# One decoder layer in fp32: the t3 splits ahead of the first pair's products, and the down projection in groups of 2, 3, 4, 3, 4, 3, 3

## The chip, the core and the metric

The kernel runs on one core of one Trainium2 chip. The core has a matrix engine (PE), a vector engine (DVE), a scalar engine (ACT), a general engine (POOL) and a queue that issues DMA (SP). Each engine takes its own instructions in the order of the program, and they wait for one another through semaphores. The metric is the device time of one execution in microseconds (us).

## The reference

The layer modulates x, adds two attention mixers, and then does what matters here: a gated feed-forward block with a residual and a layer norm.

```python
u = x * (1.0 + scale_f) + shift_f                  # (1024, 1024)
h = jnp.einsum('btd,df->btf', u, w_gate_up)        # 2 x 2816 columns
hg, hu = jnp.split(h, 2, axis=-1)
y = jnp.einsum('btf,fd->btd', jax.nn.silu(hg) * hu, w_down)
x = layer_norm(DEEPNORM_ALPHA * x + (1.0 + gate_f) * y, ln2_g, ln2_b)
```

Everything is float32.

## The kernel before

A float32 product is made from rounded halves. An operand is split into a high part (ACT copies it to fp32r) and a low part (DVE subtracts the high part from the operand), and a product takes three matmuls: high with high, high with low, low with high. A split is thus one ACT and one DVE instruction, and both must be done before the matmuls that read it.

The 2816 hidden columns are 22 blocks of 128, called f or p. The program has two stages here.

**Gate and up, 22 pairs p.** For each pair the gate and up columns come from seven products of half size instead of eight (a Strassen-like scheme). `PRODUCTS = ("b11", "b21", "t2", "t1", "t3", "b22", "t4")` names the seven right-hand operands, i = 0 to 6. Each is an array of four 128-row blocks k, with a high and a low tile (t3h and t3l, and so on). They are made once, around the first pair, from the normalised activations: `late_input(k)` and `late_rest(name, k)` make and split block k. The left-hand operand of product i of pair p is a combination of weight halves, split by `g_split(p, i)` into w_hi and w_lo, four buffers each. POOL makes the combinations in `g_sums(p, step)`. Each product is 12 matmuls over four blocks k. For pairs 0 to 2, products 0 and 1 are made ahead of the loop over p; the first pair's products 2 to 6 are the first work of that loop, and the DVE and ACT instructions of `late_rest` stand between them. `g_prepare(upto)` splits the weights of the next products ahead of their use. The result of pair p is stored to HBM (h_d).

**Down, groups of f.** `groups = [3] * 6 + [4]` are the numbers of blocks f in a group. For each group, for each of eight row blocks tb and each of two halves eh, PE sums 3 matmuls per f into one PSUM bank (`ps_f` has six banks), and DVE adds the bank to the sum zt in SBUF (line 1326). While a group runs, the arrays of the next one are made at certain row blocks: `h_prepare(f)` splits h, which `h_load(f)` fetched from HBM, and two `ws.step()` split the two halves of w_down of that f. A `ws.step()` has POOL multiply the raw weights by the gate (line 62), ACT and DVE split them (lines 78 and 79), and SP fetch a later piece into one of three raw buffers. The first group's arrays are made during the last pair (p = 21). Groups alternate between two pools of big tiles, `bigu` with 8 and `low` with 6; an f takes two tiles.

In the last group DVE also takes the statistics of each finished row block and applies the norm (`half_stats`, `moments`, `norm_shared`; `norm_quick` for the last block). The line that decides at which row blocks arrays are made is

```python
if todo and tb % 2 == 0 or len(todo) > 3 - tb // 2 and todo:
```

that is row blocks 0, 2, 4 for three blocks f and 0, 2, 4, 6 for four.

Of the kernel before, what the change touches and what calls it, by code (L numbers as in the profile page):

```python
# [98 lines left out]
def decoder_layer(ctx: ExitStack, tc: tile.TileContext, I, out, dbg=None):  # L99
    nc = tc.nc  # L100
# [83 lines left out]
            add_chunk(I["w_o"][eh, kp], 2, 1, lambda eh=eh: gates[2][:, eh * 512:(eh + 1) * 512],  # L184
                      pair_dest(late, kp, lambda kp: "low", "o_hl") if eh else None)
    ws.limit = len(ws.jobs)
    down_pool = lambda f: "low" if min(f // 3, 6) % 2 else "bigu"
    for f in range(NF):
        for c in range(2):
            ws.add(I["w_down"][f * P:(f + 1) * P, c * 512:(c + 1) * 512], 1,  # L190
# [904 lines left out]
    def g_split(p, i):  # L1095
        hi, lo = [wpool.tile([P, 512], F32R, name=s, tag=s, bufs=4) for s in ("w_hi", "w_lo")]
        split(hi, lo, g_source(p, i))
        ready.append((hi, lo))
# [60 lines left out]
    def late_rest(name, k):  # L1159
        r12, r22 = late[k]  # L1160
        if name == "t1":
            split_to("t1", k, raw11[:, k])
            nc.gpsimd.tensor_tensor(r12, r22, r12, op=OP.subtract)
        elif name == "t3":
            split_to("t3", k, r12)
        elif name == "b22":
            split_to("b22", k, r22)
        else:
            split_to("t4", k, raw21[:, k])
# [20 lines left out]
            early_gate(k // 2)  # L1190
    late_rest("t1", 3)
    g_split(0, 3)


    jobs = [(p, i) for p in range(NF) for i in range(2 if p < EARLY_PAIRS else 0, 7)]
    prepared = [2]

    def g_prepare(upto):
        while prepared[0] < min(upto, len(jobs)):
# [4 lines left out]
            prepared[0] += 1  # L1204


    groups = [3] * 6 + [4]
    hs, h_raw = {}, {}

    def h_load(f):  # L1210
# [8 lines left out]
    for p in range(NF):  # L1219
        ps = dict(zip("ab", acc.pop(p))) if p in acc else {}  # L1220
        if p == 1:
            x2_ctx.close()
            ev = ctx.enter_context(tc.tile_pool(name="ev", bufs=1, side="right", reuse_waits="tile"))
        s, g = {}, [None, None]

        def kept(name):
            if p:
                return ev.tile([P, TH], F32, name=name, bufs=4 if name == "g" else 1)
            return x2p.tile([P, TH], F32, name="r", tag="r", bufs=6)

        for i in range(7):
            if p == 0 and i == 2:
                late_rest("t3", 0)
                early_gate(2)
            elif (p, i) in jobs:
                g_prepare(n + 3)
            bank = "abacaca"[i]
            if bank not in ps:
                ps[bank] = ps_f.tile([P, TH], F32, name="pf")
            if (p, i) in jobs:  # L1240
                product(ps[bank], i, i in (0, 1, 3))
                n += 1
            x = ps[bank]
            if i in (0, 2):
                g[i // 2] = gated.get(p) if i == 0 else None
                if not g[i // 2]:
                    g[i // 2] = kept("g")
                    nc.scalar.activation(g[i // 2], x, AF.Copy)
            if p == 0 and i == 2:
                for k in range(1, 4):  # L1250
                    late_rest("t3", k)
                operand("t4", low)
                g_prepare(n + 2)
            if i in (3, 4):
                s[i] = kept(f"c{i}")
                nc.scalar.activation(s[i], x, AF.Copy)
            if i in (1, 5):
                t = i // 5
                if t or p not in gated:
                    nc.vector.tensor_tensor(g[t], g[t], x, op=OP.add)  # L1260
                nc.scalar.activation(g[t], g[t], AF.Silu)
            if i == 4:
                nc.gpsimd.tensor_tensor(s[4], s[4], s[3], op=OP.add)
            if i == 6:
                nc.vector.tensor_tensor(g[0], g[0], x, op=OP.mult)
                nc.vector.tensor_tensor(g[1], g[1], s[4], op=OP.mult)
                for t in range(2):
                    nc.sync.dma_start(h_d[p][:, t * TH:(t + 1) * TH], g[t])
            if p == 0 and i in (3, 4):
                for k in range(4):  # L1270
                    if i == 3:
                        nc.vector.tensor_tensor(raw21[:, k], raw21[:, k], raw_t2[:, k], op=OP.subtract)
                    late_rest({3: "b22", 4: "t4"}[i], k)
            if p + 1 < NF:
                if i == 4 and p + 2 < NF:
                    g_load(p + 2)
                if i in (2, 3, 4):
                    g_sums(p + 1, i - 2)
                if p == NF - 2 and i == 5:
                    ws.limit = None  # L1280
                    ws.send()
            else:
                if i == 0:
                    h_load(0)
                    h_load(1)
                    for j in range(3):
                        ws.scale(len(ws.done) + j)
                if i in (2, 3, 4):
                    h_prepare(i - 2)
                    if i == 2:  # L1290
                        h_load(2)
                for _ in range({2: 2, 3: 1, 5: 1, 6: 2}.get(i, 0)):
                    ws.step()
            if p == EARLY_PAIRS and i == 0:
                gb1 = norm_params(1)
            if i == 6 and EARLY_PAIRS <= p < EARLY_PAIRS + NB:
                gain(p - EARLY_PAIRS, gb1)
# [4 lines left out]
    for gi, n in enumerate(groups):  # L1302
        fs = range(f0, f0 + n)
        f0 += n
        last = gi == len(groups) - 1
        todo = [] if last else list(range(f0, f0 + groups[gi + 1]))
        for f in todo[:2]:
            if f not in h_raw:
                h_load(f)
        for tb in range(NB):  # L1310
            c = slice(tb * P, (tb + 1) * P)
            if todo and tb % 2 == 0 or len(todo) > 3 - tb // 2 and todo:
                f = todo.pop(0)
                h_prepare(f)
                ws.step()
                ws.step()
                if len(todo) > 1:
                    h_load(todo[1])
            for eh in range(2):
                es = slice(eh * 512, (eh + 1) * 512)  # L1320
                pd = ps_f.tile([P, TH], F32, name="pf")
                for i, f in enumerate(fs):
                    wd, h = wd_t[f][0], hs[f]
                    mac(pd, (h[:, 0, c], h[:, 1, c]), (wd[:, 0, es], wd[:, 1, es]), i == 0, i == n - 1)
                z = zrow(tb)[:, es]
                nc.vector.scalar_tensor_tensor(z, z, ALPHA if gi == 0 else 1.0, pd, op0=OP.mult, op1=OP.add)  # L1326
                if last:
                    half_stats(tb, eh)
                    if eh == 0 and tb:
                        ends.pop(0)()  # L1330
            if last:
                if tb == NB - 1:
                    norm_quick(tb, gb2, out)
                else:
                    ends.append(norm_shared(tb, gb2, out))
# [77 lines left out]
```

## Time and profile before

| | |
|---|---|
| median of 3 runs | 1901.1 us (1900.1 to 1901.41) |
| the profiled execution, its own time | 1908.77 us |
| its span from the first to the last instruction | 1907.0 us |
| mean granted TensorE clock | 0.987 of full |
| PE busy | 1841.1 us (97%) |
| DVE / ACT / POOL busy | 1160.4 / 782.0 / 596.5 us |

The profiled execution is 7.7 us longer than the median of the runs without a profile. Times below are microseconds from the start of its span. Matmuls overlap, so the step from one start to the next tells the rate, not the duration of one.

### The profile page before, as it was taken

The page shows a single profiled execution, that of the slowest core. Times are in us where ns is not written, and L with a number is a line of the kernel's source. Part 1 is how long each engine was busy: PE and PEld are TensorE (multiplying, and loading weights), DVE is VectorE, ACT ScalarE, POOL GpSimd, SP SyncE. Part 2 cuts the span into 40 slices and gives each one's busy share as a digit, 9 for nine tenths or more (in the row PEclk, how much of TensorE's full clock was granted, in tenths as well). Part 3 has the DMA queues.
Part 4 walks back from the last instruction along what each step waited for, and adds up shares of the span by engine and source line. Part 5 has one row for each costly group of instructions (what it writes and reads, how often), then busy time and mean ns, then how long its engine had stood idle before and what let it go on. Part 6 is the DMA issues. An engine that isn't in the chain of part 4 may idle for free.

```text
span 1907.0 us, 24471 instructions
## 1 busy us (share of the span) xinstructions
PE 1841.1 (97%) x8988; PEld 1489.6 (78%) x8988; DVE 1160.4 (61%) x2161; ACT 782.0 (41%) x1661; POOL 596.5 (31%) x389
## 2 busy tenths in 40 slices
PE   6899999999999999989999999999999999899998
PEld 5688877878878777768888878778888888788886
DVE  7855667667677887534555364575565444565557
ACT  3455545445444767633122132653333333412122
POOL 2432223223323222100311142455664333431213
PEclk9899999999999999989999999999999999999999
DMA  8011112111121122254534123123222222432222
GB/s 316 28 34 34 40 41 74 45 57 56 41 63 50 53 89 68 79 178 164 175 118 161 56 75 124 56 89 100 89 78 89 78 89 95 135 125 90 93 71 89
DMA packets 72266, 170.83 MB, mean 90 GB/s; under 512 B 13073, under 2 KB 14161, under 8 KB 72146
## 3 DMA queue, kind: packets, MB, share of 16 engines
q1 hardware_dynamic: 71810, 168.21, 26.7%
q8 instruction: 71, 1.16, 0.3%
q0 software_dynamic: 336, 1.06, 0.2%
q14 instruction: 49, 0.40, 0.1%
HBM read 145.80 MB, written 23.43 MB: 89 GB/s over the span
## 4 chain that ended last, share of the span: by engine, by line
PE 51%; DVE 3%; ACT 1%; issue 1%; DMA 1%; SPq 0%; POOL 0%; DVEq 0%; ACTq 0%; POOLq 0%
PE pf L1106 21%; PE p L138 5%; PE p L139 5%; PE p L137 5%; PE pf L137 5%; PE pf L139 5%; PE pf L138 5%; DVE m L118 1%; DMA h_raw<-h_d 0%; DVE wd L79 0%; DVE h L118 0%; DMA oa_d<-o 0%; PE px L1034 0%; PE p L835 0%; PE p L842 0%
## 5 line engine op out<-in xcount | busy, mean ns | idle before, releaser
L137 PE MATMUL pj<-u,w_hi 128*128 128x512 f32 x720 | 301.5, 419 | 0.0
L139 PE MATMUL pj<-u,w_lo 128*128 128x512 f32 x720 | 283.9, 394 | 0.0
L138 PE MATMUL pj<-u,w_hi 128*128 128x512 f32 x720 | 282.6, 392 | 0.0
L425 POOL TENSOR_TENSOR rb<-rb,sin_t 128x512 f32<-128x512 f32 x64 | 86.8, 1356 | 502.0 <-DVE rb L423 431.5
L118 DVE TENSOR_TENSOR w_lo<-r,w_hi 128x512 fp32r<-128x512 f32 x110 | 117.7, 1072 | 138.7 <-ACT w_hi L117 137.9
L79 DVE TENSOR_TENSOR w_lo<-w_raw,w_hi 128x512 fp32r<-128x512 f32 x150 | 133.4, 893 | 85.3 <-ACT w_hi L78 83.0
L528 ACT ACTIVATE probs<-probs,st 128x128 f32<-128x128 f32 (+1 forms) x320 | 146.0, 461 | 60.5 <-DVE st L518 30.8
L137 PEld LDWEIGHTS pj<-u,w_hi 128*128 128x128 f32 x720 | 136.4, 189 | 33.6 <-issue 4.7
L139 PEld LDWEIGHTS pj<-u,w_lo 128*128 128x128 f32 x720 | 135.8, 189 | 30.7
L138 PEld LDWEIGHTS pj<-u,w_hi 128*128 128x128 f32 x720 | 136.7, 190 | 22.6
L137 PE MATMUL pf<-wd,h 128*128 128x512 f32 x352 | 139.2, 395 | 3.4 <-DVE zt L1326 2.9
L138 PE MATMUL pf<-wd,h 128*128 128x512 f32 x352 | 138.7, 394 | 1.9 <-DVE wd L79 1.9
L139 PE MATMUL pf<-wd,h 128*128 128x512 f32 x352 | 138.6, 394 | 0.0
L62 POOL TENSOR_TENSOR w_raw<-w_raw,gate 128x512 f32<-128x512 f32 x60 | 83.1, 1404 | 157.0 <-DMA w_raw<-in_w_down 134.4
L1326 DVE SCALAR_TENSOR_TENSOR zt<-zt,pf 128x512 f32<-128x512 f32 x112 | 76.2, 685 | 85.1 <-PE pf L139 85.0
L426 POOL TENSOR_TENSOR r<-ra,rb 128x512 f32<-128x512 f32 x63 | 114.5, 1817 | 6.1 <-DVE kl L460 1.3
L78 ACT ACTIVATE w_hi<-w_raw 128x512 fp32r<-128x512 f32 x150 | 92.0, 624 | 29.0 <-PE p L138 12.0
L552 ACT ACTIVATE ptsb<-pt 128x512 f32<-128x512 f32 (+1 forms) x128 | 63.6, 548 | 93.6 <-PE pt L550 93.2
L137 PE MATMUL p<-u,w_hi 128*128 128x512 f32 x224 | 88.3, 394 | 0.0
L139 PE MATMUL p<-u,w_lo 128*128 128x512 f32 x224 | 87.2, 389 | 0.0
L138 PE MATMUL p<-u,w_hi 128*128 128x512 f32 x224 | 87.2, 389 | 0.0
L137 PE MATMUL p<-o_hl,w_hi 128*128 128x512 f32 x192 | 75.9, 395 | 8.0 <-ACT o_hl L117 8.0
(297 smaller groups left out, 4267.2 us busy)
## 6 DMA issues: line engine op xcount, KB each, us to landing
w_raw<-in_w_in SPq DMA_DIRECT2D x118, 256.0 KB
r<-in_w_gate_up SPq DMA_DIRECT2D x47, 512.0 KB
a_raw<-in_w_ada SPq DMA_DIRECT2D x32, 512.0 KB
w_raw<-in_w_down SPq DMA_DIRECT2D x44, 256.0 KB
h_raw<-h_d SPq DMA_DIRECT2D x22, 512.0 KB
h_d<-g SPq DMA_DIRECT2D x40, 256.0 KB
wa<-in_w_ada_m SPq DMA_DIRECT2D x16, 512.0 KB
wb<-wt_d SPq DMA_DIRECT2D x24, 256.0 KB
```

The source lines that it names most:

```text
L62: self.nc.gpsimd.tensor_tensor(self.raws[i], self.raws[i], scale(), op=OP.mult)
L78: self.nc.scalar.activation(hi, raw, AF.Copy)
L79: self.nc.vector.tensor_tensor(lo, raw, hi, op=OP.subtract)
L118: nc.vector.tensor_tensor(lo, src, hi, op=OP.subtract)
L137: nc.tensor.matmul(ps, w[0], m[0], start=first, stop=False)
L138: nc.tensor.matmul(ps, w[0], m[1], start=False, stop=False)
L139: nc.tensor.matmul(ps, w[1], m[0], start=False, stop=last)
L425: eng.tensor_tensor(b, b, sin_t[:, s], op=OP.mult)
L426: eng.tensor_tensor(residue_half(res, r, t), by_residue(a, r), by_residue(b, r), op=OP.add)
L528: nc.scalar.activation(pr, pr, AF.Exp, bias=st[:, 0, h, b:b + 1], accum_out=st[:, 1, h, b:b + 1])
L1106: nc.tensor.matmul(ps, w[:, c], m[:, k], start=first and k == 0 and n == 0, stop=k == 3 and n == 2, skip_group_check=True)
L1326: nc.vector.scalar_tensor_tensor(z, z, ALPHA if gi == 0 else 1.0, pd, op0=OP.mult, op1=OP.add)
```

## The change

Three things are changed. First, the four splits of t3, and the weight split of product 4 of pair 0, stand before the loop over pairs, so ahead of the first pair's products 2 and 3 in the program; before, one t3 split stood ahead of product 2 and three behind it. Second, the first Silu of pair 0 stands behind that of its second half (i = 5). Third, the down groups are 2, 3, 4, 3, 4, 3, 3, the last pair makes the arrays of two blocks f instead of three (and loads the raw h of blocks 2 and 3), and the next group's arrays are made at row blocks 1, 3, 5 for three and 1, 2, 4, 6 for four.

```diff
--- before.py
+++ after.py
@@ -184,7 +184,8 @@
             add_chunk(I["w_o"][eh, kp], 2, 1, lambda eh=eh: gates[2][:, eh * 512:(eh + 1) * 512],
                       pair_dest(late, kp, lambda kp: "low", "o_hl") if eh else None)
     ws.limit = len(ws.jobs)
-    down_pool = lambda f: "low" if min(f // 3, 6) % 2 else "bigu"
+    groups = [2, 3, 4, 3, 4, 3, 3]
+    down_pool = lambda f: "low" if sum(f >= e for e in np.cumsum(groups)) % 2 else "bigu"
     for f in range(NF):
         for c in range(2):
             ws.add(I["w_down"][f * P:(f + 1) * P, c * 512:(c + 1) * 512], 1,
@@ -1190,10 +1191,15 @@
             early_gate(k // 2)
     late_rest("t1", 3)
     g_split(0, 3)
+    for k in range(2):
+        late_rest("t3", k)
+    g_split(0, 4)
+    for k in range(2, 4):
+        late_rest("t3", k)
 
 
     jobs = [(p, i) for p in range(NF) for i in range(2 if p < EARLY_PAIRS else 0, 7)]
-    prepared = [2]
+    prepared = [3]
 
     def g_prepare(upto):
         while prepared[0] < min(upto, len(jobs)):
@@ -1204,7 +1210,6 @@
             prepared[0] += 1
 
 
-    groups = [3] * 6 + [4]
     hs, h_raw = {}, {}
 
     def h_load(f):
@@ -1230,7 +1235,6 @@
 
         for i in range(7):
             if p == 0 and i == 2:
-                late_rest("t3", 0)
                 early_gate(2)
             elif (p, i) in jobs:
                 g_prepare(n + 3)
@@ -1247,10 +1251,7 @@
                     g[i // 2] = kept("g")
                     nc.scalar.activation(g[i // 2], x, AF.Copy)
             if p == 0 and i == 2:
-                for k in range(1, 4):
-                    late_rest("t3", k)
                 operand("t4", low)
-                g_prepare(n + 2)
             if i in (3, 4):
                 s[i] = kept(f"c{i}")
                 nc.scalar.activation(s[i], x, AF.Copy)
@@ -1258,7 +1259,10 @@
                 t = i // 5
                 if t or p not in gated:
                     nc.vector.tensor_tensor(g[t], g[t], x, op=OP.add)
-                nc.scalar.activation(g[t], g[t], AF.Silu)
+                if p or t:
+                    nc.scalar.activation(g[t], g[t], AF.Silu)
+            if p == 0 and i == 5:
+                nc.scalar.activation(g[0], g[0], AF.Silu)
             if i == 4:
                 nc.gpsimd.tensor_tensor(s[4], s[4], s[3], op=OP.add)
             if i == 6:
@@ -1285,11 +1289,10 @@
                     h_load(1)
                     for j in range(3):
                         ws.scale(len(ws.done) + j)
-                if i in (2, 3, 4):
-                    h_prepare(i - 2)
-                    if i == 2:
-                        h_load(2)
-                for _ in range({2: 2, 3: 1, 5: 1, 6: 2}.get(i, 0)):
+                if i in (2, 4):
+                    h_prepare(i // 2 - 1)
+                    h_load(i // 2 + 1)
+                for _ in range({2: 2, 3: 1, 5: 1}.get(i, 0)):
                     ws.step()
             if p == EARLY_PAIRS and i == 0:
                 gb1 = norm_params(1)
@@ -1304,12 +1307,13 @@
         f0 += n
         last = gi == len(groups) - 1
         todo = [] if last else list(range(f0, f0 + groups[gi + 1]))
+        prepare_at = {0: (), 3: (1, 3, 5), 4: (1, 2, 4, 6)}[len(todo)]
         for f in todo[:2]:
             if f not in h_raw:
                 h_load(f)
         for tb in range(NB):
             c = slice(tb * P, (tb + 1) * P)
-            if todo and tb % 2 == 0 or len(todo) > 3 - tb // 2 and todo:
+            if tb in prepare_at:
                 f = todo.pop(0)
                 h_prepare(f)
                 ws.step()
```

DVE at the first pair. Names are those of the tiles (w_lo is the low part of a weight, raw and raw_t are the unsplit t4 and t2). Before:

```order
L118 TENSOR_TENSOR w_lo<-s_10415,w_hi 128x512
L1047 TENSOR_TENSOR t3l<-r,t3h 128x512
L1175 TENSOR_TENSOR spare<-spare,pf 128x512
L1047 TENSOR_TENSOR t3l<-r,t3h 128x512 x2
L1047 TENSOR_TENSOR t3l<-spare,t3h 128x512
L118 TENSOR_TENSOR w_lo<-r_10350,w_hi 128x512
L118 TENSOR_TENSOR w_lo<-r_10348,w_hi 128x512
L1272 TENSOR_TENSOR raw_10061<-raw_10061,raw_t_10487 128x512
```

and with the change:

```order
L118 TENSOR_TENSOR w_lo<-s_10415,w_hi 128x512
L1048 TENSOR_TENSOR t3l<-r,t3h 128x512 x2
L118 TENSOR_TENSOR w_lo<-r_10350,w_hi 128x512
L1048 TENSOR_TENSOR t3l<-r,t3h 128x512
L1048 TENSOR_TENSOR t3l<-spare,t3h 128x512
L1176 TENSOR_TENSOR spare<-spare,pf 128x512
L118 TENSOR_TENSOR w_lo<-r_10348,w_hi 128x512
L1276 TENSOR_TENSOR raw_10061<-raw_10061,raw_t_10487 128x512
```

The same eight rows of work stand there; the weight split of product 4 (w_lo<-r_10350) is third or fourth instead of sixth, and the addition that reads PSUM (spare<-spare,pf) comes last of the moved ones.

DVE at the end of the last pair and in the first down group, before:

```order
L118 TENSOR_TENSOR h<-h_raw,h 128x1024
L1260 TENSOR_TENSOR g<-g,pf 128x512
L79 TENSOR_TENSOR wd<-w_raw,wd 128x512
L1265 TENSOR_TENSOR g<-g,pf 128x512
L1266 TENSOR_TENSOR g<-g,c_13717 128x512
L79 TENSOR_TENSOR wd<-w_raw,wd 128x512 x2
L118 TENSOR_TENSOR h<-h_raw,h 128x1024
L79 TENSOR_TENSOR wd<-w_raw,wd 128x512 x2
L1326 SCALAR_TENSOR_TENSOR zt<-zt,pf 128x512 x4
```

and with the change:

```order
L118 TENSOR_TENSOR h<-h_raw,h 128x1024
L1261 TENSOR_TENSOR g<-g,pf 128x512
L79 TENSOR_TENSOR wd<-w_raw,wd 128x512
L1269 TENSOR_TENSOR g<-g,pf 128x512
L1270 TENSOR_TENSOR g<-g,c_13714 128x512
L1330 SCALAR_TENSOR_TENSOR zt<-zt,pf 128x512 x2
L118 TENSOR_TENSOR h<-h_raw,h 128x1024
L79 TENSOR_TENSOR wd<-w_raw,wd 128x512 x2
L1330 SCALAR_TENSOR_TENSOR zt<-zt,pf 128x512 x4
```

Before, the splits of w_down for the third f and those of the fourth f's h and weights stand ahead of the first addition of a down bank (L1326); now two such additions come first, and no weight split of the running group is behind the last pair.

SP's queue in the same place, before:

```order
L1212 DMA h_raw<-h_d 128x1024 x3
L55 DMA w_raw<-in_w_down 128x512 x4
L1268 DMA h_d<-g 128x512 x2
L55 DMA w_raw<-in_w_down 128x512 x2
L921 DMA gb<-in_ln_g 128x1024
L921 DMA gb<-in_ln_b 128x1024
L1212 DMA h_raw<-h_d 128x1024 x2
```

and with the change:

```order
L1217 DMA h_raw<-h_d 128x1024 x3
L55 DMA w_raw<-in_w_down 128x512 x3
L1217 DMA h_raw<-h_d 128x1024
L55 DMA w_raw<-in_w_down 128x512
L1272 DMA h_d<-g 128x512 x2
L922 DMA gb<-in_ln_g 128x1024
L922 DMA gb<-in_ln_b 128x1024
L55 DMA w_raw<-in_w_down 128x512 x2
L1217 DMA h_raw<-h_d 128x1024
```

The load of the fourth h has moved ahead of the loads of the norm's parameters (gb); two pieces of w_down that stood ahead of gb are behind it.

## Rows read from the trace of the kernel before

**Rows 1.** The page's first part: busy time, share of the span and instructions of each engine.

```profile
PE 1841.1 (97%) x8988; PEld 1489.6 (78%) x8988; DVE 1160.4 (61%) x2161; ACT 782.0 (41%) x1661; POOL 596.5 (31%) x389
```

**Rows 2.** The windows view: a stretch, its length, the busy time of each engine (instructions), the granted clock of TensorE as a share of full, the share of DMA engines busy, GB/s.

```profile
1249.00:1254.00 5.00, 5.00 (x12) 3.95 (x13) 5.00 (x9) 1.79 (x4) 0.00 (x0) 0.50 0.31 105
...
1654.00:1657.00 3.00, 3.00 (x8) 2.35 (x8) 0.00 (x0) 0.00 (x0) 1.28 (x1) 0.50 0.91 284
...
1668.00:1674.00 6.00, 5.76 (x14) 4.51 (x15) 5.85 (x7) 1.59 (x3) 3.94 (x2) 0.50 0.51 177
...
1680.00:1855.00 175.00, 175.00 (x773) 144.91 (x773) 96.00 (x136) 35.91 (x49) 39.53 (x31) 1.00 0.28 95
```

**Rows 3.** The timeline of PE over the first pair's products 2 to 6 and the first matmul behind them (start, duration, engine, line, operation, out<-in; in brackets the idle time before it and what ended it).

```profile
1237.74 0.39 PE L1106 MATMUL pf<-t2h,w_hi 128*128 128x512 f32 x1
...
1244.27 0.40 PE L1106 MATMUL pf<-t1h,w_lo 128*128 128x512 f32 x1
1246.81 0.50 PE L1106 MATMUL pf<-t3h,w_hi 128*128 128x512 f32 x1 [2.14 <-ACT w_hi L117]
...
1248.90 0.80 PE L1106 MATMUL pf<-t3h,w_lo 128*128 128x512 f32 x1 [1.35 <-DVE w_lo L118]
...
1259.36 0.39 PE L1106 MATMUL pf<-t2h,w_hi 128*128 128x512 f32 x1
```

**Rows 4.** The timeline of DVE over the same stretch; rows of one kind that follow at once are merged (x2, x4).

```profile
1241.34 0.68 DVE L118 TENSOR_TENSOR w_lo<-s,w_hi 128x512 fp32r<-128x512 f32 x1
1243.24 0.76 DVE L1047 TENSOR_TENSOR t3l<-r,t3h 128x512 fp32r<-128x512 f32 x1 [1.22 <-ACT t3h L1046]
...
1245.24 2.40 DVE L1047 TENSOR_TENSOR t3l<-r,t3h 128x512 fp32r<-128x512 f32 x2 [0.64 <-ACT t3h L1046]
...
1254.79 2.48 DVE L1047 TENSOR_TENSOR t4l<-raw,t4h 128x512 fp32r<-128x512 f32 x4
```

**Rows 5.** The timeline of POOL over the same stretch.

```profile
1242.15 1.30 POOL L1080 TENSOR_TENSOR s<-r 128x512 f32<-128x512 f32 x1 [2.49 <-issue]
...
1245.22 1.27 POOL L1082 TENSOR_TENSOR s<-s,r 128x512 f32<-128x512 f32 x1
1254.24 4.79 POOL L1263 TENSOR_TENSOR r<-r 128x512 f32<-128x512 f32 x1 [7.76 <-ACT r L1256]
1259.00 1.29 POOL L1084 TENSOR_TENSOR r<-r,r 128x512 f32<-128x512 f32 x1
```

**Rows 6.** The view of the tiles wd: the matmuls of the down projection by line (count, duration in ns min/median/max, first and last start in us).

```profile
L137 PE MATMUL pf<-wd,h x352: 389/389/793, 1648.3 to 1897.7; 128*128 128x512 f32 x176
...
L139 PE MATMUL pf<-wd,h x352: 388/389/632, 1648.8 to 1898.1; 128*128 128x512 f32 x176
```

**Rows 7.** The timeline of PE in the first down group.

```profile
1649.46 0.39 PE L139 MATMUL pf<-wd,h 128*128 128x512 f32 x1
1650.34 0.50 PE L137 MATMUL pf<-wd,h 128*128 128x512 f32 x1 [0.49 <-ACT wd L78]
1652.78 0.50 PE L138 MATMUL pf<-wd,h 128*128 128x512 f32 x1 [1.94 <-DVE wd L79]
...
1664.98 0.39 PE L139 MATMUL pf<-wd,h 128*128 128x512 f32 x1
1668.24 0.79 PE L137 MATMUL pf<-wd,h 128*128 128x512 f32 x1 [2.88 <-DVE zt L1326]
```

**Rows 8.** The timelines of SP (two rows), ACT and DVE in the first down group.

```profile
1653.74 1.76 SPq L921 DMA_DIRECT2D gb<-in_ln_g  x1
...
1656.03 1.15 SPq L1212 DMA_DIRECT2D h_raw<-h_d  x2
...
1664.07 1.06 ACT L117 ACTIVATE h<-h_raw 128x1024 fp32r<-128x1024 f32 x1 [13.03 <-DMA h_raw<-h_d]
...
1667.51 2.47 DVE L1326 SCALAR_TENSOR_TENSOR zt<-zt,pf 128x512 f32<-128x512 f32 x4
```

**Rows 9.** The timeline of DVE in the last down group, a little more than one row block's work.

```profile
1869.35 0.70 DVE L929 BATCH_NORM_STATS2 bst<-zt 128x6 f32<-128x512 f32 x1
1869.96 1.21 DVE L960 TENSOR_TENSOR zt<-zt,gb 128x1024 f32<-128x1024 f32 x1
1871.34 0.69 DVE L1326 SCALAR_TENSOR_TENSOR zt<-zt,pf 128x512 f32<-128x512 f32 x1 [0.18 <-PE pf L139]
1872.07 0.69 DVE L929 BATCH_NORM_STATS2 bst<-zt 128x6 f32<-128x512 f32 x1
1872.79 0.21 DVE L934 BATCH_NORM_AGGREGATE bmv<-bst 128x2 f32<-128x12 f32 x1
1873.04 0.15 DVE L936 TENSOR_SCALAR brs<-bmv 128x1 f32<-128x1 f32 x1
1873.46 0.16 DVE L955 RECIPROCAL brs<-brs 128x1 f32<-128x1 f32 x1 [0.27 <-ACT brs L937]
1873.66 0.16 DVE L956 SCALAR_TENSOR_TENSOR brs<-bmv,brs 128x1 f32<-128x1 f32 x1
1874.06 0.69 DVE L1326 SCALAR_TENSOR_TENSOR zt<-zt,pf 128x512 f32<-128x512 f32 x1 [0.24 <-PE pf L139]
```

**Rows 10.** POOL beside the rows above.

```profile
1871.24 2.40 POOL L961 TENSOR_TENSOR zt<-zt,gb 128x1024 f32<-128x1024 f32 x1 [3.04 <-DVE zt L960]
```

**Rows 11.** DVE's last addition of a down bank.

```profile
1898.54 0.69 DVE L1326 SCALAR_TENSOR_TENSOR zt<-zt,pf 128x512 f32<-128x512 f32 x1 [0.18 <-PE pf L139]
```

## Prediction

> **What bounds the kernel now.** The page's first part says PE: busy 97% of the span [rows 1]. So time is lost only where PE waits or runs at half clock. I looked for such places with the windows view. From 1680 to 1855 us the clock is full and PE busy throughout: 773 matmuls, one cut off at an edge, in 175.0 us, a step of 0.227 us [rows 2]. At half clock 12 matmuls took 5.0 us, 0.42 us a step [rows 2]. The change touches two lossy places and one that is not.
>
> *First pair.* The 60 matmuls of products 2 to 6 run from 1237.74 to 1259.36 [rows 3]: 21.6 us, where 60 x 0.227 = 13.6 would do. 8.0 us are lost. The waits named there are for w_hi (2.14) and w_lo (1.35) of product 4 [rows 3], and behind them the clock is half [rows 2].
>
> *First down group.* 1056 matmuls, 352 on each of three lines, start between 1648.3 and 1898.1 [rows 6]: 249.8 us for 1055 steps, where 239.2 would do. 10.6 us are lost, all before 1680. Two gaps hold 5.9 of it: 1649.46 to 1652.78 with one matmul between (3.3 less two steps), where PE waits for the third block's w_down, and 1664.98 to 1668.24 (3.3 less one step), where it waits for DVE to add a bank [rows 7]. The rest, 4.7, is half clock after each gap (1654 to 1657, 1668 to 1674) [rows 2]. The second gap starts far back: SP issued the fourth h behind the norm's parameters at 1656.03, ACT could take it only at 1664.07, DVE's additions are queued behind its split and came at 1667.51 [rows 8], and the six banks were full.
>
> *Last down group.* PE does not wait. DVE does, a little: it waits for PE 0.18 and 0.24 us in each row block [rows 9]. A block of four f is 24 matmuls, 5.44 us; DVE needs not much less.
>
> **The change, part by part.**
>
> *Down stalls removed: -10.6.* With two blocks f in the first group nothing of the third is needed before PE has passed 8 x 12 matmuls, 21.8 us, so the first gap goes. The third and fourth h are loaded in the last pair, ahead of the norm's parameters, so the wait that ended at 1664.07 goes too, and with both gaps their half clock. Next late is the fourth block's second piece of w_down, now fetched behind the parameters. SP's queue was moving 284 GB/s at a 0.91 share there [rows 2], and it must move about 2.75 MB (two halves of h, 1 MB of parameters, three pieces, one h) from about 1651.5 on: 9.7 us, to 1661. Behind that piece stand another and the h, 0.77 MB or 2.7 us, so it lands near 1658.5; POOL, ACT and DVE take some 2.6 us more (1.3, 0.6 and 0.7), to 1661. DVE's additions are queued behind it from row block 3 on. PE needs the seventh bank, six banks of 6 matmuls (1.36 us) after the end of row block 2, at 1648.3 + 12 x 1.36 = 1664.6. That leaves 3.6 us of cover; without it each microsecond later would be one lost. I put 0.3 for what may stick out, with bounds of 0 and 3.
>
> *Last group with three f instead of four: +6.8.* A row block is now 18 matmuls, 4.08 us. DVE's work in it, from start to start and without its waits for PE, is: addition 0.73, statistics 0.61, the multiplication with the gain of the block before 1.13 (1.38 less 0.18 of waiting, less an overlap of 0.08), addition 0.73, statistics 0.72, then 0.25, 0.42, 0.20 and 0.16 for the small ones [rows 9]. The sum is 4.95. So DVE becomes the bound of this group. Counted from the group's start: the second addition of block 0 at 4.08 + 0.19, its block ends 2.48 later at 6.75, six more blocks of 4.95 end at 36.45, and the last block's second addition comes 0.73 + 0.61 + 1.13 later, at 38.9. PE's last bank is there at 32.6 + 0.2. The kernel's end hangs on that last addition, which stood 0.4 us behind the last matmul [rows 6, 11]; it is 6.1 us later against PE's end. POOL adds to this: its 2.40 us addition starts right behind DVE's multiplication [rows 9, 10] and ends 2.47 us behind it, while DVE's small instruction with two SBUF inputs (line 956) would be due 2.24 us behind it. If it is held, six blocks cost 0.23 each, 1.4 in all. Bounds 6.1 and 7.5; I take 6.8. The bank count does not stop PE, but PE ending early is worth nothing.
>
> *Middle groups: 0.* The number of matmuls and additions is the same. A row block of three f gives DVE 4.08 us for two additions (1.2) and, where arrays are made, one h and two w_down splits (an estimate of 2.4 at 0.60 for 512 columns); a block of four gives more. The cover is PE's own 4.08 us; with POOL in the way (two instructions of 1.3) it would be gone, but six banks of 2.04 hold 12 us.
>
> *t3 splits moved: +0.6.* No instruction is added; one Silu moves. DVE's queue from 1241.34 to the last t4l is 21 instructions (w_lo, four t3l, the addition of spare, two w_lo, eight for raw and b22l, w_lo, four t4l). At 0.60 each (2.48 for four) that is 12.6, ending at 1253.9; before it ended at 1257.2 [rows 4]. The 3.3 between are waits for t3h (1.22 and 0.64) and time behind POOL (two t3l took 2.40, not 1.28) [rows 4]. If all of it went and PE followed at full clock 0.7 us behind, instead of 2.1, 4.8 us would be gained. But three POOL instructions, about 3.8 us, lie in the same stretch [rows 5]. DVE's 1245.24 row shows a split held until POOL's 1245.22 row was through [rows 4, 5]. Before, most of POOL's time fell into DVE's waits; now there are none, and only the addition that reads PSUM (0.6) can lie under POOL. So 3.2 come back, and DVE ends at 1257.1, where it was. What remains is PE's shorter tail, -1.5. Against that: product 4 ends some 4 us earlier, so POOL's lines 1263 and 1084 become due inside the b22 and t4 splits. Before, line 1263 waited from 1254.24 to about 1257.7 while DVE ran on, taking 4.79 us for work of 1.3, and line 1084 came at 1259.00, behind the t4 splits [rows 5]. If they take turns with DVE, 2.5 more fall on it. Two Silu on ACT now stand ahead of a w_hi of pair 1, and PE, fed one b22 block in 1.2 us for 0.68 us of work, may fall to half clock: up to 2 together. Bounds -4.8 and +3. Both kinds of meeting stand in the rows (DVE held once, POOL held once); between -1.5 and +3 I take +0.6.
>
> The Trainium skill (SBUF — State Buffer, Who interferes with whom) says that a DVE instruction with two SBUF inputs and a GpSimd (POOL) one that reads SBUF exclude each other, and that the one that issues first has the pair for its whole instruction. By that rule line 1263 would have had to wait for one DVE instruction only; the trace shows it waiting through six. By the rule this part is +2.4 and the sum -1.1; by the row at 1254.24 it is about -0.5 and the sum -4.0.
>
> *Sum.* -10.6 + 0.3 + 6.8 + 0.6 = -2.9. On the profiled execution that is a span of 1904.1 instead of 1907.0. Its own time, 1908.8, is 7.7 above the median of the runs, 1901.1, so I apply the difference to the median: 1898.2 us, 0.15% less. Less than 0.2% (3.8 us) can't be told from no change here.
>
> **Rivals.**
>
> 1. *The last group costs nothing.* If DVE's period were 4.1 and not 4.95, the sum would be -9.7: 1891.4. Against it: each of the nine terms stands in the rows. Chance 0.08.
>
> 2. *The t3 move pays.* If POOL's three instructions get out of DVE's way, up to -4.8 instead of +0.6: -8.3, 1892.8, or 1895 with half of it. For it: at 1254.24 POOL did wait. Against it: product 5's w_lo itself waits for POOL's second instruction. Chance 0.15.
>
> 3. *POOL takes turns with DVE everywhere.* +2.4 instead of +0.6: 1900.0. For it: DVE's 1245.24 row. Against it: POOL's 1254.24 row. Chance 0.22.
>
> 4. *Slower: the first group stalls anew.* The place is row block 3, the price one microsecond for each that the fourth block's second piece lands after about 1662, and from some 3 us of gap on the half clock as before (4.7 for two gaps). At a landing of 1666 the stall is about 4 and the clock costs 2.5: -2.9 + 6.5 = +3.6, near 1904.7; from there on it is slower. For it: the fourth h took 8 us behind the parameters [rows 8]. Against it: the piece stands ahead of a 512 KB h and needs less. Chance 0.08.
>
> That the change does not do what it says, I leave out: the order of the queues shows that it does.
>
> **How the numbers follow.** The forecast has 0.47, with a range of its own from 1896 to 1900.5. The time is its value, 1898.2. The range of 8 in 10 reaches into rivals 2 and 3 and leaves out rival 1, the better half of rival 2 and most of rival 4: 1894.0 to 1902.5. Faster (below 1897.3): rival 1 (0.08), most of rival 2 (0.13) and the lower end of the forecast (0.12), 0.33. Slower (above 1904.9): most of rival 4, 0.07. Same: 0.60.
>
> **What would show it.** In the first down group no PE wait over 1 us and full clock. In the last group PE without waits, DVE's additions drifting from PE's banks by about 0.9 us a row block, and the last addition 6 to 8 us behind the last matmul. In the first pair, product 4 earlier by 2 us or more, but new PE waits for b22l, and the first matmul of pair 1 within 2 us of 1259.4. The forecast is wrong if DVE keeps pace in the last group, if b22l comes without a wait, or if a wait for w_down stands at row block 3.

## The result and the profile after

| | median | lowest to highest | runs |
|---|---|---|---|
| before | 1900.88 us | 1899.09 to 1902.91 | 20 |
| after | 1903.22 us | 1900.77 to 1909.63 | 20 |

The ratio after to before is 1.0013, with an interval of 1.0007 to 1.0019. So the changed kernel is 2.3 us slower (1.3 to 3.6 by the interval). That is within the 0.2% that the prediction called no change, but the time lies outside its range, 0.7 us above the upper end. The profiled execution of the changed kernel took 1901.34 us, with a span of 1899.5.

Compared naively, the two profiles tell the opposite: spans of 1907.0 and 1899.5, a gain of 7.5 us. The page's first part shows PE 7.7 us less busy than in [rows 1], with as many matmuls; that is the first sign that the two executions didn't run at the same clock. The profiled execution of the kernel before is 7.9 us above the median of its kernel and that of the changed kernel 1.9 us below its own, so the two together show a gain that the timed runs don't have.

```profile
PE 1833.4 (97%) x8988; PEld 1484.0 (78%) x8988; DVE 1166.8 (61%) x2161; ACT 781.9 (41%) x1661; POOL 595.4 (31%) x389
```

**The first down group.** The windows view of the changed kernel, over the stretch from the first to the 73rd matmul of the down projection. The columns are those of [rows 2].

```profile
1644.71:1661.03 16.32, 16.32 (x73) 13.51 (x72) 13.09 (x19) 6.03 (x9) 7.43 (x6) 1.00 0.62 203
```

72 steps at 0.227 us are 16.3, and that is what they took: both gaps of [rows 7] are gone, and the clock is full. The same 72 steps of the kernel before:

```profile
1648.32:1675.29 26.97, 21.66 (x73) 16.58 (x72) 13.77 (x18) 8.08 (x12) 9.83 (x7) 0.81 0.54 176
```

Profile against profile, the removed stall is thus 26.97 - 16.32 = 10.65 us, the prediction's figure to a tenth.

**The last down group.** The chain of work that ended last in the changed kernel (start, length, engine, tile, line; five of its pieces):

```profile
1856.43 0.70 DVE bst L930
1859.51 1.21 DVE zt L961
...
1884.68 1.21 DVE zt L961
1889.66 1.21 DVE zt L961
1892.63 1.75 DVE zt L945
```

From 1855.7 to the end the chain is DVE's, but for a piece of 0.21 us on ACT in each row block except the last. PE has no wait in this group. The timelines of DVE and then of PE at its end:

```profile
1885.81 0.68 DVE L1330 SCALAR_TENSOR_TENSOR zt<-zt,pf 128x512 f32<-128x512 f32 x1
...
1890.79 0.68 DVE L1330 SCALAR_TENSOR_TENSOR zt<-zt,pf 128x512 f32<-128x512 f32 x1
```

```profile
1883.84 0.39 PE L139 MATMUL pf<-wd,h 128*128 128x512 f32 x1
```

The last matmul starts 14.3 us earlier than in [rows 6], the last addition only 7.75 us earlier than in [rows 11]: it now stands 6.95 us behind the last matmul, where it stood 0.44 behind. So PE's early end is given back, 6.5 us of it, as the prediction said. The two additions are one row block apart: 4.98 us, against 4.95 forecast and 4.08 of PE's work.

**The first pair.** PE's timeline at products 4 (t3) and 5 (b22) in the changed kernel:

```profile
1240.71 0.50 PE L1107 MATMUL pf<-t3h,w_lo 128*128 128x512 f32 x1 [0.98 <-DVE w_lo L118]
...
1243.66 0.39 PE L1107 MATMUL pf<-b22h,w_hi 128*128 128x512 f32 x1
1246.49 0.50 PE L1107 MATMUL pf<-b22l,w_hi 128*128 128x512 f32 x1 [2.44 <-DVE b22l L1048]
...
1248.79 0.79 PE L1107 MATMUL pf<-b22l,w_hi 128*128 128x512 f32 x1 [1.33 <-DVE b22l L1048]
```

Of the waits of 2.14 and 1.35 that stood at product 4 [rows 3] a wait of 0.98 is left, and waits of 2.44 and 1.33 stand at product 5. DVE, then POOL, over the same stretch:

```profile
1236.59 2.38 DVE L1048 TENSOR_TENSOR t3l<-r,t3h 128x512 fp32r<-128x512 f32 x2
1238.90 1.76 DVE L118 TENSOR_TENSOR w_lo<-r,w_hi 128x512 fp32r<-128x512 f32 x1
1240.58 1.78 DVE L1048 TENSOR_TENSOR t3l<-r,t3h 128x512 fp32r<-128x512 f32 x1
...
1244.69 1.75 DVE L1048 TENSOR_TENSOR b22l<-r,b22h 128x512 fp32r<-128x512 f32 x1
1246.36 1.77 DVE L1276 TENSOR_TENSOR raw<-raw,raw_t 128x512 f32<-128x512 f32 x1
...
1251.67 2.48 DVE L1048 TENSOR_TENSOR t4l<-raw,t4h 128x512 fp32r<-128x512 f32 x4
```

```profile
1236.80 1.63 POOL L1081 TENSOR_TENSOR s<-r 128x512 f32<-128x512 f32 x1 [2.48 <-issue]
1238.37 1.74 POOL L1087 TENSOR_TENSOR r<-r,s 128x512 f32<-128x512 f32 x1
1240.19 1.62 POOL L1083 TENSOR_TENSOR s<-s,r 128x512 f32<-128x512 f32 x1
1244.54 1.35 POOL L1267 TENSOR_TENSOR r<-r 128x512 f32<-128x512 f32 x1 [2.73 <-ACT r L1257]
1245.85 1.73 POOL L1085 TENSOR_TENSOR r<-r,r 128x512 f32<-128x512 f32 x1
```

Five POOL instructions, and beside each one DVE instruction that takes some 1.1 us more than its 0.68 (in the first row, a pair that takes 2.38 instead of 1.28). In the kernel before one was held in this way [rows 4]. DVE's four t4 splits start 19.3 us behind the first matmul of product 2 (at 1232.38); before, they started 17.1 us behind it [rows 3, 4]. The first matmul of pair 1 comes 22.6 us behind it, where it came 21.6 behind.

So the places and the waits came out as forecast, and the sum did not. The question is which size was wrong.

### The profile page after: what moved, and what is told of

Read it like the earlier page. It is cut to its first block, busy times and chain, and to the rows that moved or that the text cites. A ratio compares the mean times of both kernels' runs of the same rounds, so it can differ in the third digit from the quotient of the medians.

```text
span 1899.5 us, 24476 instructions
## 1 busy us (share of the span) xinstructions
PE 1833.4 (97%) x8988; PEld 1484.0 (78%) x8988; DVE 1166.8 (61%) x2161; ACT 781.9 (41%) x1661; POOL 595.4 (31%) x389
## 4 chain that ended last, share of the span: by engine, by line
PE 49%; DVE 5%; issue 1%; ACT 1%; DMA 0%; POOL 0%; DVEq 0%; ACTq 0%; POOLq 0%
PE pf L1107 21%; PE p L138 5%; PE p L139 5%; PE p L137 5%; PE pf L139 4%; PE pf L137 4%; PE pf L138 4%; DVE m L118 1%; DVE bst L930 1%; DVE zt L1330 0%; DVE zt L961 0%; DVE w_lo L118 0%; PE px L1035 0%; DVE t3l L1048 0%; DVE raw L1276 0%
## 5 line engine op out<-in xcount | busy, mean ns | idle before, releaser
L137 PE MATMUL pf<-wd,h 128*128 128x512 f32 x352 | 136.9, 389 | 0.0
L138 PE MATMUL pf<-wd,h 128*128 128x512 f32 x352 | 136.9, 389 | 0.0
L139 PE MATMUL pf<-wd,h 128*128 128x512 f32 x352 | 136.9, 389 | 0.0
```

What stands on the lines that cost most here:

```text
L137: nc.tensor.matmul(ps, w[0], m[0], start=first, stop=False)
L138: nc.tensor.matmul(ps, w[0], m[1], start=False, stop=False)
L139: nc.tensor.matmul(ps, w[1], m[0], start=False, stop=last)
```

## The experiments

Theory A after the result: the 10.6 us were read from one execution that was 7.9 us longer than the median of its kernel, and the part of them that is half clock isn't there in others. Theory B, the rival: the stall is worth 10.6, and the first pair gives back some 5 us more than forecast. The later runs put a narrower question each, and their A and B are those of their own text.

**The t3 part alone.** The first pair as changed, the groups as before:

```diff
+    for k in range(2):
+        late_rest("t3", k)
+    g_split(0, 4)
+    for k in range(2, 4):
+        late_rest("t3", k)
...
-    prepared = [2]
+    prepared = [3]
...
-                nc.scalar.activation(g[t], g[t], AF.Silu)
+                if p or t:
+                    nc.scalar.activation(g[t], g[t], AF.Silu)
+            if p == 0 and i == 5:
+                nc.scalar.activation(g[0], g[0], AF.Silu)
```

> Only the t3 part and the moved Silu; the down groups are those of before. Theory A (the three terms have the size that the two profiled executions show, except that the stall in the first down group was larger in the profiled execution of before than it usually is): the first pair is longer by 1.75 us, as between the two profiles (the lead at the first t2 matmul, 5.36, has shrunk to 3.61 at the first down matmul), so about +1.8 us, 1902.7 against 1900.9. Theory B (the down terms hold as predicted, -10.6 and +6.8, and the first pair usually costs more than in the one profile): +5 to +6 us, about 1906.5.

Measured: 1900.92 us against 1900.41, ratio 1.0009 (1.0000 to 1.0018): +0.5 by the medians, +1.7 by the ratio (0 to 3.4). B's 5 us are not there. Its first down group is that of before, gaps and all, yet its 72 steps took 22.22 us and not 26.97:

```profile
1645.19:1667.41 22.22, 17.19 (x74) 13.36 (x73) 11.09 (x15) 6.04 (x10) 8.38 (x7) 1.00 0.62 201
```

**The groups alone.** The first pair as before, groups 2, 3, 4, 3, 4, 3, 3 with their arrays where the change puts them:

```diff
-    groups = [3] * 6 + [4]
+    groups = [2, 3, 4, 3, 4, 3, 3]
...
-                if i in (2, 3, 4):
-                    h_prepare(i - 2)
-                    if i == 2:
-                        h_load(2)
-                for _ in range({2: 2, 3: 1, 5: 1, 6: 2}.get(i, 0)):
+                if i in (2, 4):
+                    h_prepare(i // 2 - 1)
+                    h_load(i // 2 + 1)
+                for _ in range({2: 2, 3: 1, 5: 1}.get(i, 0)):
...
-            if todo and tb % 2 == 0 or len(todo) > 3 - tb // 2 and todo:
+            if tb in prepare_at:
```

> Only the down groups 2, 3, 4, 3, 4, 3, 3 with their row blocks and the last pair's loads; the first pair is that of before. Theory A: the stall removed is worth about 6 us in a usual execution (the median moved by +2.3, less 1.75 for the first pair, less 6.8 for the last group), so about +0.6 us, 1901.5. Theory B: -10.6 + 6.8 = -3.8 us, 1897.1.

Measured: 1900.74 us against 1900.41, ratio 1.0000 (0.9991 to 1.0008). The groups gain nothing as a whole; a stall of 10.6 less 6.8 would have been -3.8, a ratio of 0.9980, outside the interval. That speaks for A.

**The same with four f in the last group.**

```diff
-    groups = [2, 3, 4, 3, 4, 3, 3]
+    groups = [2, 3, 4, 3, 3, 3, 4]
```

> As the run with the groups alone, but the groups are 2, 3, 4, 3, 3, 3, 4, so that the last one again has four blocks. If the last group of three is what costs, this is faster than the groups alone by 6.8 us. Theory A: -6 us against before, about 1895. Theory B: -10.6 us, about 1890. If DVE's drift in the last group costs nothing, it equals the run with the groups alone.

Measured: 1893.84 us against 1900.41, ratio 0.9963 (0.9949 to 0.9976). The last group is that of before, and in the profile the 1055 steps of the down projection take 239.13 us, full clock from end to end; so this is what the stall is worth in timed runs: 6.6 us by the medians, 7.0 by the ratio (4.6 to 9.7). 10.6 would be a ratio of 0.9944, just below the interval. The kernel is faster than both kernels of this case. Its last matmul, on PE, and its last addition, on DVE:

```profile
1883.21 0.39 PE L139 MATMUL pf<-wd,h 128*128 128x512 f32 x1
```

```profile
1883.64 0.69 DVE L1326 SCALAR_TENSOR_TENSOR zt<-zt,pf 128x512 f32<-128x512 f32 x1 [0.18 <-PE pf L139]
```

The addition stands 0.43 us behind the matmul, as in the kernel before. Against the groups alone, moving the four from the fifth place of the list to the last is worth 6.9 us.

**Only the last group made smaller.** The fifth group takes the block that the last one gives up (and the choice of the tile pool follows the list); all else as before:

```diff
-    groups = [3] * 6 + [4]
+    groups = [3, 3, 3, 3, 4, 3, 3]
...
```

> The kernel before with the groups 3, 3, 3, 3, 4, 3, 3: nothing changes but that the last group has three blocks and the fifth four. It measures the last group by itself. Both theories: DVE's 4.95 us a row block against PE's 4.08 make the end 6.1 to 7.5 us later, about +6.8, 1907.7. If DVE's drift costs nothing: 0.

Measured: 1907.67 us against 1900.41, ratio 1.0037 (1.0024 to 1.0049): +7.3. The last group costs what was forecast. This run, too, keeps the first group of before, with all three waits, but the clock stays full. PE's waits there, and the windows view of the 72 steps:

```profile
1646.62 0.50 PE L137 MATMUL pf<-wd,h 128*128 128x512 f32 x1 [0.49 <-ACT wd L78]
1649.07 0.50 PE L138 MATMUL pf<-wd,h 128*128 128x512 f32 x1 [1.94 <-DVE wd L79]
1662.89 0.50 PE L137 MATMUL pf<-wd,h 128*128 128x512 f32 x1 [2.87 <-DVE zt L1326]
```

```profile
1644.61:1667.10 22.49, 17.18 (x73) 13.35 (x72) 11.07 (x15) 6.01 (x10) 8.31 (x7) 1.00 0.62 199
```

These are the waits of [rows 7] almost to a hundredth (0.49, 1.94, 2.88). Yet the loss is 22.49 - 16.3 = 6.2 us and not 10.65.

**The kernel before, once more.** No edit, one execution.

> The kernel before, unchanged, profiled once more. Theory A (the 4.7 us of half clock in the first down group belonged to that one profiled execution): the first 72 matmuls of the down projection start over 22.2 to 22.5 us, as in the two experiments that kept its first group, against 27.0 in the profile shown; both gaps are there, the granted clock of the stretch is about 1.00, the loss 5.9 to 6.2 us, and the span about 1899. Theory B (the half clock belongs to the kernel): 27.0 us again, clock 0.81 over the stretch, loss 10.6.

Measured: 1902.03 us, span 1900.3. The 72 steps:

```profile
1646.26:1668.54 22.28, 18.85 (x74) 14.50 (x72) 11.13 (x15) 6.08 (x10) 8.40 (x7) 0.92 0.61 201
```

and its last wait there:

```profile
1664.29 0.50 PE L137 MATMUL pf<-wd,h 128*128 128x512 f32 x1 [0.98 <-DVE zt L1326]
```

The loss is 6.0 us. Theory A holds in the sum; in the clock it was too simple: here the mean is 0.92, so some half clock did come after the first gap, and in exchange the second wait is 0.98 instead of 2.88, which would fit a slower PE that reaches the full banks later (argued, not shown). This accounts for the whole difference between the two executions of one program: the down projection starts 2.06 us earlier (1646.26 and 1648.32), the 72 steps are 4.69 us shorter, together 6.75, and the spans differ by 6.7.

**One load moved in the kernel before.** The raw h of block 3 ahead of the norm's parameters:

```diff
                     h_prepare(i - 2)
-                    if i == 2:
-                        h_load(2)
+                    if i in (2, 4):
+                        h_load(i // 2 + 1)
```

> The kernel before with its groups of three, and one load moved: the raw h of block 3 is fetched in the last pair, ahead of the norm's parameters, instead of behind them. Theory A (the second gap of the first down group starts at that load): the second gap, 3.0 us between two matmuls in the usual execution, goes, the first one (the wait for the third block's w_down, 2.9 us with its two steps) stays, and the time is 2.6 to 3.0 us less, about 1897.6 us; so the smaller first group is worth the other half of the 6 us. Theory B (the fourth block's pieces of w_down, still behind the parameters, keep DVE's additions back as before): the second gap stays at 2 to 3 us and the time is within 1 us of the kernel before.

Measured: 1898.23 us against 1899.77, ratio 0.9990 (0.9981 to 0.9999). PE's one wait over 1 us in the first group, and the 72 steps:

```profile
1647.32 0.50 PE L138 MATMUL pf<-wd,h 128*128 128x512 f32 x1 [1.95 <-DVE wd L79]
```

```profile
1642.86:1663.78 20.92, 18.48 (x73) 14.58 (x72) 14.77 (x19) 8.31 (x12) 9.43 (x7) 0.92 0.62 200
```

The second gap is gone, as theory A said: it did start at the load that SP issued late. The gain is 1.5 us by the medians and 1.9 by the ratio; the interval, 0.2 to 3.6, doesn't exclude the 2.6 to 3.0 that were expected. The one trace shows a loss of 4.6 in which 2.9 is the first gap and the rest half clock behind it. So one gap less is not yet the clock back: what a half clock costs behind the gap that stays differs from one execution to another.

**The changed kernel with four f in the last group.**

```diff
-    groups = [2, 3, 4, 3, 4, 3, 3]
+    groups = [2, 3, 4, 3, 3, 3, 4]
```

> The changed kernel with four blocks f in its last group (groups 2, 3, 4, 3, 3, 3, 4). Theory A (the t3 part costs 2.1 to 2.4 us, as the traces of the first pair say): the groups' -6.5 and the t3 part's +2.2 give -4.3, about 1896.1 us. Theory B (the t3 part costs 0.5 us, as the median of the run with it alone says): -6.0, about 1894.4 us.

Measured: 1896.83 us against 1900.36, ratio 0.9976 (0.9965 to 0.9986). The only difference from the last-four kernel above (ratio 0.9963) is the t3 part with its moved Silu: 0.0013, or 2.5 us. That is nearer to theory A, but theory B's -6.0, a ratio of 0.9968, lies within the interval too, so the times don't decide. The traces below do.

**Without three sums of POOL, in the changed kernel and in the one before.** Pair 1's weight sums are left out; it takes those of pair 0. The same edit in both, one execution each:

```diff
-                if i in (2, 3, 4):
+                if p == 0 and i == 2:
+                    sums_w[1] = sums_w[0]
+                if p and i in (2, 3, 4):
                     g_sums(p + 1, i - 2)
```

> The changed kernel without three of POOL's instructions in the first pair: the weight sums of pair 1 are left out (pair 1 takes the sums of pair 0). Theory A (POOL takes turns with DVE, and this is what the moved t3 splits lose): five DVE instructions of the first pair that took 1.75 to 1.78 us instead of 0.68 become two, DVE reaches its last t4 split about 3.2 us earlier, and the loss of the first pair's 60 matmuls against full clock falls from 9.8 to about 6.6 us. Theory B (DVE's row of instructions is too long whatever POOL does, or ACT is late): the waits for the low part of b22 stay within 1 us of 2.8 and 1.7, and the loss within 1 us of 9.8.

> The same three POOL instructions left out of the kernel before. Theory A: only one DVE instruction was held there (1.79 instead of 0.68), so the first pair gains at most 1.1 us: loss 6.6 to 7.7 instead of 7.7. Theory B: if POOL costs both kernels alike, the gain is the same as in the changed kernel.

The two executions took 1899.48 us (changed) and 1899.93 us. The measure is the time of 132 matmuls from the first of the first pair's product 2: the 60 of its products 2 to 6, the same 60 of pair 1, and the 12 of pair 2's product 2 (products 0 and 1 of these pairs were made ahead). At full clock they would take 29.9 us. (The 9.8 and 7.7 of the expectations are the losses over these 132; over the 60 alone they are 9.0 and 8.0 in the two profiles.) The windows view of the changed kernel, of the kernel before, and of the two without the sums (changed, before):

```profile
1232.38:1272.07 39.69, 33.73 (x133) 24.77 (x132) 33.98 (x39) 22.78 (x40) 19.91 (x13) 0.96 0.21 73
```

```profile
1237.74:1275.68 37.94, 33.81 (x133) 26.32 (x132) 30.36 (x39) 22.56 (x40) 22.22 (x13) 0.91 0.22 77
```

```profile
1233.11:1270.13 37.02, 33.39 (x133) 25.27 (x132) 30.75 (x39) 22.46 (x40) 15.25 (x10) 0.95 0.23 79
```

```profile
1235.36:1271.11 35.75, 33.38 (x134) 25.26 (x133) 29.78 (x40) 22.58 (x40) 20.47 (x10) 0.95 0.23 82
```

All three executions with the t3 part (the change, the t3 part alone, four f last in the changed kernel) take 39.69; the six with the old order take 37.45 to 38.20, 37.76 in the mean. Behind these 132 matmuls every one of the nine takes 372.64 us to the first down matmul. So the t3 part costs 1.9 us, and all of it stands here.

Without the sums the changed order gains 2.7 us and the old one 2.0, and the difference falls from 1.9 to 1.3. In the changed order this is about theory A (a loss of 7.1, where 6.6 was expected and B said 8.8 to 10.8). In the old order the gain was to be 1.1 at most, and that was wrong: POOL's sums cost both orders nearly the same, and leaving them out takes away only a third of the difference. The edit isn't a clean one either: in both kernels POOL's next instruction comes earlier and holds a t1 split, so that PE waits for the w_lo of product 3 longer than before (0.56 and 0.54). On PE, changed and then before:

```profile
1238.57 0.79 PE L1107 MATMUL pf<-t1h,w_lo 128*128 128x512 f32 x1 [1.64 <-DVE w_lo L118]
```

```profile
1240.83 0.80 PE L1106 MATMUL pf<-t1h,w_lo 128*128 128x512 f32 x1 [1.66 <-DVE w_lo L118]
```

What is left of the difference stands in two places. The first is product 5. Changed kernel without the sums, on PE, DVE and POOL:

```profile
1249.28 0.50 PE L1107 MATMUL pf<-b22l,w_hi 128*128 128x512 f32 x1 [1.34 <-DVE b22l L1048]
```

```profile
1246.85 1.78 DVE L1276 TENSOR_TENSOR raw<-raw,raw_t 128x512 f32<-128x512 f32 x1
```

```profile
1246.44 1.64 POOL L1267 TENSOR_TENSOR r<-r 128x512 f32<-128x512 f32 x1 [9.69 <-ACT r L1257]
```

The old order without the sums, on PE and POOL:

```profile
1250.80 0.50 PE L1106 MATMUL pf<-b22l,w_hi 128*128 128x512 f32 x1 [0.23 <-DVE b22l L1047]
```

```profile
1248.69 6.82 POOL L1263 TENSOR_TENSOR r<-r 128x512 f32<-128x512 f32 x1 [9.66 <-ACT r L1256]
```

In the changed order POOL's addition of two products takes its turn among the b22 splits: one DVE instruction is 1.1 us longer, and PE waits 1.34 for b22l instead of 0.23. In the old order the same addition is held until DVE's run of splits is through. Over the 60 matmuls of the first pair the difference is 0.8 us.

The second place, with 0.5 us, is product 4 of pair 1, and there the moved Silu has a part. ACT and DVE in the changed kernel without the sums (the moved Silu is line 1265), then DVE in the old order:

```profile
1254.01 0.62 ACT L1265 ACTIVATE w_raw<-w_raw 128x512 f32<-128x512 f32 x1
1254.53 0.62 ACT L117 ACTIVATE w_hi<-s 128x512 fp32r<-128x512 f32 x1
```

```profile
1255.18 0.69 DVE L118 TENSOR_TENSOR w_lo<-s,w_hi 128x512 fp32r<-128x512 f32 x1 [1.75 <-ACT w_hi L117]
```

```profile
1256.17 0.69 DVE L118 TENSOR_TENSOR w_lo<-s,w_hi 128x512 fp32r<-128x512 f32 x1 [1.22 <-ACT w_hi L117]
```

The Silu stands ahead of this w_hi, and DVE waits half a microsecond longer for it. The w_lo of pair 1's product 4 stands behind this split in DVE's queue, and PE waits for it, where the old order shows no wait:

```profile
1259.55 0.50 PE L1107 MATMUL pf<-t3h,w_lo 128*128 128x512 f32 x1 [0.29 <-DVE w_lo L118]
```

DVE's t4 splits show the same sum (changed order, then old):

```profile
1249.75 2.49 DVE L1048 TENSOR_TENSOR t4l<-raw,t4h 128x512 fp32r<-128x512 f32 x4
```

```profile
1251.26 2.50 DVE L1047 TENSOR_TENSOR t4l<-raw,t4h 128x512 fp32r<-128x512 f32 x4
```

They start 16.6 and 15.9 us behind the first matmul of product 2: 0.7 later, and with the 0.5 of the Silu 1.3. That these two places make the remaining 1.3 is read from the rows; neither was taken away by itself.

## Why the prediction was wrong

**"Down stalls removed: -10.6" was mis-sized; it is -6.0 to -6.6.** The term had two parts: 5.9 in gaps, each with an instruction that PE waited for, and "the rest, 4.7, is half clock after each gap". The gaps are in every execution that keeps the first group of before. The half clock of that length was in one of five: the loss over the 72 steps was 10.7 in the execution shown, and 5.9, 6.0, 6.2 and 6.3 in the t3 part alone, before once more, last three, and before without the sums. Timed, the stall is worth 6.6 (last four; 4.6 to 9.7 by the interval). The prediction noted that its execution was 7.7 us longer than the median, and then applied the difference of that execution to the median of others. The excess was not spread over the whole span, as this assumed: 4.7 of it lay in the very term that was being priced. The removal itself went as its steps said: no wait over 1 us and full clock in the first group, and nothing stuck out (the +0.3 was 0, and rival 4 did not come).

**"Last group with three f: +6.8" was right.** 6.5 in the profile at the last addition, 6.9 between the groups alone and last four, 7.3 in last three. The sum of DVE's instructions in a row block, 4.95, met 4.98.

**"t3 splits moved: +0.6" was mis-sized; it is +1.9 in the traces and 0.5 to 3.0 in times** (0.5 and 3.0 by medians, 1.7 and 2.5 by ratios, from the t3 part alone and from the two kernels with four f last). Product 4 does come 7.7 us earlier in the profile (5.4 of which it had gained before, since its first product also starts earlier: 1232.38 against 1237.74, so 2.3 by the change), and the new waits for b22l are there, as announced. The step that failed is the choice between the two kinds of meeting. The prediction had POOL's first three instructions hold DVE for 3.2 us, and so they do. For the other two (lines 1267 and 1085, 1263 and 1084 before) it had "If they take turns with DVE, 2.5 more fall on it", and took +0.6, about midway. They do take turns: both hold a DVE instruction, and DVE's t4 splits start 2.2 us later against product 2, where the forecast without turns was "DVE ends at 1257.1, where it was". This is what rival 3 described, and its price of +2.4 was close. How much of the 1.9 each hold costs PE isn't shown: without three of the five the difference is still 1.3, half a microsecond of it behind the moved Silu, which the prediction had named too. The Trainium skill (SBUF — State Buffer, Who interferes with whom) says that a DVE instruction with two SBUF inputs contends with a GpSimd (POOL) one that reads SBUF, and that the lock on the ports they share is exclusive; the four rows of 1.75 to 1.78 agree. I had set this aside for one row of 4.79 in which POOL waited instead [rows 5].

**The sum.** -6.6 + 6.9 + 1.9 = +2.2, with the stall and the last group from times and the t3 part from traces; measured, +2.3. The three terms have an uncertainty of a microsecond or more each in times, so that the sum meets so closely is in part luck. Of the 5 us between 1898.2 and 1903.2, 4.0 to 4.6 is the stall, 1.3 the t3 part, and the 0.3 that did not stick out goes the other way.

**Left open.** Why the clock was half for so long in one execution of the first group, and for less or hardly at all in others with the same waits, was not found out. Nor was the moved Silu tried by itself, nor each of POOL's five instructions.

## What to carry to other kernels

When the profiled execution is longer than the median of the timed runs by more than the effect that is priced, first find where the excess lies: the part of a loss that is waits named in rows comes again, while half clock behind a gap may not, so bound it by zero below. Before moving DVE work into a stretch where POOL is active, count POOL's instructions there, since in the new order each of the five held DVE for about 1.1 us. When work is regrouped, give the last group enough matmuls to cover the vector work that only it has: the place of the four in the list was worth 6.9 us here.

## What the runs showed of the hardware

The same waits are not always followed by the same clock: after waits of 0.49, 1.94 and 2.9 us the clock over the first 72 steps was 0.81 in one execution and 1.00 in another, with a difference of 4.5 us for one and the same work.

POOL's addition of two products met DVE's runs of splits in two ways. At line 1263 of the old order it took 4.79 us [rows 5], 4.78 to 5.37 in the six executions, and 6.82 without the sums, held until the splits were through; at line 1267 of the changed order it took 1.32 to 1.35 in three executions and 1.64 without the sums, and held DVE instead. No run here shows what decides which of the two waits.
